# A masked softmax: VectorE's unrolled work put into a loop, and sixteen small writes of the output taken out

## The chip, the cores and the metric

The kernel runs on one core of one Trainium2 chip. The metric is the time of one execution in device microseconds.

## The reference, cut to what matters

```python
batch, heads, seq_q, seq_k = 16, 8, 256, 256
# lengths: 16 integers, each from 128 to 255
for b in range(batch):
    length = lengths[b]
    masked = x[b, :, :, :length]
    e = np.exp(masked - masked.max(-1, keepdims=True))
    result[b, :, :, :length] = e / e.sum(-1, keepdims=True)   # zeros past length
```

A batch is 2048 rows of 256 float32, 2.1 MB, and lies in SBUF as 128 partitions of 16 rows. Input and output are 33.6 MB each; the kernel reads only the columns that a batch needs, rounded up to a width.

## The kernel before

There are eight slots for batches in SBUF. SyncE issues the loads of the first four batches and all stores, GpSimd issues the loads of the later twelve (each of a width picked by the length). VectorE clips what lies past the length to a huge negative number, ScalarE takes the exponential and the row sums, VectorE takes the reciprocals and multiplies. The parts that the argument touches:

```python
# the small writes: one piece of 64 bytes in each of 16 places of the first batch's output
nc.vector.memset(touch, 0.0).then_inc(s_zero, 1)
nc.scalar.wait_ge(s_zero, 1)
nc.scalar.dma_start(out=out_e, in_=touch).then_inc(s_touch, 16)
...
# SyncE: the stores; `parts` cuts batches 0 to 9 in a half and two quarters
nc.sync.wait_ge(s_touch, 16)
for b in range(batch):
    s_b = s_st[b % 2]
    for s in parts(b):
        nc.sync.wait_ge(s_out, ...)                  # VectorE has finished this part
        if b >= 2 and s.start == 0:
            nc.sync.wait_ge(s_b, 64 * (b // 2 + 1))  # the store of batch b-2 has landed
        nc.sync.dma_start(out=out_f[b, :, s, :], in_=xt[:, b % slots, s, :])...
...
# VectorE, unrolled over 16 batches
def mask(b, s):
    v_len = length(DVE, word[0:1, 2 * b : 2 * b + 1])    # reads the length into a register
    nc.vector.wait_ge(s_sw[b % 2], 16 * ((b - ahead) // 2 + 1))   # the load has landed
    with nc.vector.If(v_len < mid):
        clip(b, s, 0, mid)
    clip(b, s, mid, seq_k).then_inc(s_min, ...)
def divide(b, h):                                        # h: a half of the batch
    nc.vector.wait_ge(s_exp, 2 * b + h + 1)
    reciprocal(...)  # counts up s_v
    nc.vector.wait_ge(s_v, v)
    multiply(...)    # counts up s_out
```

The softmax here doesn't subtract the row's maximum and nothing guards it: scores larger than these inputs give would overflow.

## Time and profile before

| | before |
|---|---|
| time, median of the first 3 runs | 156.84 us (156.65 to 157.08) |
| span of the profiled run | 155.0 us |
| moved through DMA | 62.08 MB, 400 GB/s over the span |
| VectorE, ScalarE busy | 74%, 68% |
| VectorE's last multiply ends | 137.9 us |

The profile's lines are read in the prediction below.

### The profile page before, as it was taken

The numbers are of one execution on the slowest core, as the hardware profiler recorded it, in microseconds if no ns is written. First come the engines' busy times: TensorE is split into PE (matmuls) and PEld (weight loads), VectorE is DVE, ScalarE is ACT, GpSimd is POOL, SyncE is SP. The second block draws the span as 40 slices with busy tenths as digits, with TensorE's granted clock in tenths as the row PEclk, the third lists the DMA queues.
The fourth block names the chain that finished last, engine by engine and source line by source line (L and its number), as shares of the span: only waits on it lengthen the run. The fifth ranks groups of instructions, "written<-read, shape, count | busy, mean of one in ns | idle before, by whom it ended". The sixth has DMA issues, their size and how long they took to land.

```text
span 155.0 us, 1322 instructions
## 1 busy us (share of the span) xinstructions
PE 0.2 (0%) x1; PEld 0.1 (0%) x1; DVE 115.1 (74%) x85; ACT 105.2 (68%) x514; POOL 19.0 (12%) x25
## 2 busy tenths in 40 slices
PE   0000000000000000000000000000000000000000
PEld 0000000000000000000000000000000000000000
DVE  1249999957999894949889499999894999950000
ACT  3087799993989694793959488989695798800000
POOL 4910031002020201102020112020100000000000
DMA  4999999999999999999999999999999999999993
GB/s 112 421 452 419 444 309 374 417 429 435 403 409 396 411 413 407 429 407 411 410 413 420 404 419 403 408 412 412 425 405 449 420 419 429 440 435 435 416 419 129
DMA packets 10452, 62.08 MB, mean 400 GB/s; under 512 B 930, under 2 KB 1026, under 8 KB 7122
## 3 DMA queue, kind: packets, MB, share of 16 engines
q1 hardware_dynamic: 6336, 41.95, 66.2%
q0 software_dynamic: 4080, 20.12, 32.0%
q14 instruction: 2, 0.02, 0.0%
q10 hardware_dynamic: 34, 0.00, 0.0%
HBM read 28.51 MB, written 33.56 MB: 400 GB/s over the span
## 4 chain that ended last, share of the span: by engine, by line
DMA 66%; DVE 15%; issue 5%; POOLq 2%; SPq 1%; DVEq 0%
DMA xt<-in_x_dram 58%; DVE xt L231 10%; DMA out_dram<-xt 8%; DVE xt L204 5%; DVE inv_sum L228 1%; SPq L117 1%; POOLq L144 0%; POOLq L139 0%; POOLq L101 0%; SPq L119 0%; SPq L127 0%; DVEq L221 0%; POOLq L166 0%; POOLq L162 0%; POOLq L168 0%
## 5 line engine op out<-in xcount | busy, mean ns | idle before, releaser
L258 ACT ACTIVATE xt<-xt x256 | 102.4, 401 | 27.7 <-DVE xt L204 27.7
L231 DVE TENSOR_TENSOR xt<-xt,inv_sum 128x2048 f32<-128x2048 f32 x32 | 73.3, 2292 | 1.1
L204 DVE SCALAR_TENSOR_TENSOR xt<-down,len_s,xt 128x2048 f32<-128x2048 f32 (+1 forms) x17 | 37.8, 2224 | 18.3 <-DMA xt<-in_x_dram 18.2
L258 ACT ACTIVATION_READ_ACCUMULATOR xt<-xt x256 | 47.9, 187 | 0.0
L139 POOL DMA_DIRECT2D xt<-in_x_dram x12 | 12.8, 1064 | 90.0 <-DMA out_dram<-xt 50.4
L228 DVE RECIPROCAL inv_sum<-row_sum 128x8 f32<-128x8 f32 x32 | 6.3, 196 | 1.1 <-ACT xt L258 1.1
L158 POOL MEMSET xt<- 128x1536 f32 x4 | 5.3, 1386 | 1.1 <-DVE len_s L195 1.1
L250 ACT ACT_TABLE_LOAD x1 | 1.3, 1283 | 2.1 <-DVE touch L112 2.1
L112 DVE MEMSET touch<- 16x16 f32 x1 | 0.1, 72 | 1.2 <-SPq L79 1.2
L187 DVE TENSOR_SCALAR down<-iota_i 128x256 f32<-128x256 int32 x1 | 0.3, 297 | 0.3 <-POOL iota_i L150 0.3
L192 DVE CAST len_b<-word 1x16 bf16<-1x16 int32 x1 | 0.2, 163 | 0.4 <-DMA word<-in_lengths_dram 0.4
L195 DVE TENSOR_SCALAR len_s<-len_f 128x16 f32<-128x16 f32 x1 | 0.2, 173 | 0.3 <-PE len_f L174 0.3
L150 POOL IOTA iota_i<- 128x256 int32 x1 | 0.3, 331 | 0.6 <-SPq L79 0.6
L155 POOL MEMSET seed<- 1x1 f32 x2 | 0.3, 162 | 0.0
L250 ACT ACTIVATE warm<-const-float32-0.0 128x1 f32<-128x1 f32 x1 | 0.2, 203 | 0.0
L153 POOL MEMSET ones<- 1x128 bf16 x1 | 0.2, 194 | 0.0
L174 PE MATMUL len_f<-len_b,ones 1*128 1x16 bf16 x1 | 0.2, 166 | 2.6 <-DVE len_b L192 2.6
L276 POOL MEMSET const-float32-0.0<- 128x1 f32 x1 | 0.1, 98 | 0.3 <-issue 0.3
L174 PEld LDWEIGHTS len_f<-len_b,ones 1*128 1x128 bf16 x1 | 0.1, 100 | 2.6 <-POOL ones L153 2.6
L276 POOL MEMSET const-bfloat16-1.0<- 128x1 bf16 x1 | 0.1, 99 | 0.0
L276 POOL MEMSET const-uint8-127<- 128x1 uint8 x1 | 0.1, 99 | 0.0
L276 POOL MEMSET const-float32-1.0<- 128x1 f32 x1 | 0.1, 98 | 0.0
(1 smaller groups left out, 0.0 us busy)
## 6 DMA issues: line engine op xcount, KB each, us to landing
out_dram<-xt SPq DMA_DIRECT2D x16, 1024.0 KB
out_dram<-xt SPq DMA_DIRECT2D x20, 512.0 KB
xt<-in_x_dram SPq DMA_DIRECT2D x3, 2048.0 KB, 16.1
out_dram<-xt SPq DMA_DIRECT2D x3, 2048.0 KB
xt<-in_x_dram POOLq DMA_DIRECT2D x3, 1728.0 KB, 16.2
xt<-in_x_dram POOLq DMA_DIRECT2D x2, 2048.0 KB, 16.2
xt<-in_x_dram POOLq DMA_DIRECT2D x2, 1600.0 KB, 14.2
xt<-in_x_dram POOLq DMA_DIRECT2D x2, 1280.0 KB, 13.6
```

Source lines behind the costliest of these rows:

```text
L117: nc.sync.dma_start(out=xt[:, 0, s], in_=x_f[0, :, s]).then_inc(s_ld[h], 16)
L139: nc.gpsimd.dma_start(out=xt[:, slot, :, :w], in_=x_n[:, n, :, :w]).then_inc(s_sw[par], 16)
L150: nc.gpsimd.iota(iota_i, pattern=[[1, seq_k]], base=0, channel_multiplier=0).then_inc(s_iota, 1)
L155: nc.gpsimd.memset(seed[:, par : par + 1], 0.0).then_inc(s_st[par], 64)
L158: nc.gpsimd.memset(xt[:, b, :, low:], 0.0).then_inc(s_fill, 1)
L174: nc.tensor.matmul(len_f, lhsT=ones, rhs=len_b, start=True, stop=True).then_inc(s_lenf, 1)
L204: return nc.vector.scalar_tensor_tensor(out=t, in0=down[:, None, lo:hi].to_broadcast([P, s.stop - s.start, hi - lo]), scalar=len_s[:, b : ...
L228: step(nc.vector.reciprocal(out=inv_sum[:, b, s], in_=row_sum[:, b, s]))
L231: nc.vector.tensor_tensor(out=t, in0=t, in1=inv_sum[:, b, s, None].to_broadcast([P, half, seq_k]), op=ALU.mult,).then_inc(s_out, 1)
L250: nc.scalar.activation(out=warm, in_=nc.const_aps.tensor(0.0, (P, 1), F32), func=EXP)
L258: ins = nc.scalar.activation(out=e, in_=e, func=EXP, accum_out=sum_h[:, bass.ds(i, 1), j])
L276: nc = _bacc.Bacc("TRN2", target_bir_lowering=False, num_devices=1)
```

## The change

The intent is a shorter program: VectorE's work for the later twelve batches stands once, in a loop over pairs of batches, and the small writes go. Cut to its core:

```diff
-        nc.vector.memset(touch, 0.0).then_inc(s_zero, 1)
-        nc.scalar.wait_ge(s_zero, 1)
-        nc.scalar.dma_start(out=out_e, in_=touch).then_inc(s_touch, 16)
 ...
-        nc.sync.wait_ge(s_touch, 16)
 ...
-        def mask(b, s):
-            v_len = length(DVE, word[0:1, 2 * b : 2 * b + 1])
-            ... wait for the load ...
+        def mask(b, slot, s):                      # the caller waits for the load first
+            v_len = length(DVE, word[0:1, one(2 * b)])
 ...
-            nc.vector.wait_ge(s_exp, 2 * b + h + 1)
+            nc.vector.wait_ge(s_exp, 2 * b + (h + 1))      # b a register in the loop
 ...
-        for b in range(batch):
-            if b == 0: divide(0, 0)
-            if b + 1 < batch: mask(b + 1, slice(0, nt))
-            if b > 0: divide(b, 0)
-            divide(b, 1)
+        for b in range(ahead - 1):                 # batches 0 to 2, still unrolled
+            nc.vector.wait_ge(s_ld[b + 2], 16)
+            mask(b + 1, b + 1, whole)
+            ... divide both halves of b ...
+        with nc.Fori(0, (batch - ahead) // 2, 1, engines=[DVE]) as r:
+            for par in range(2):
+                n = 2 * r + (ahead + par)
+                b = 2 * r + (ahead + par - 1)
+                nc.vector.wait_ge(s_sw[par], 16 * r + 16)
+                mask(n, n % slots, whole)
+                for h in range(2):
+                    divide(b, b % slots, h)
```

More of the change, by code (lines that the diff above doesn't have):

```diff
@@ L74 @@
     warm = pool.tile([P, 1], F32, name="warm")
-    few = 16
-    touch = pool.tile([few, few], F32, name="touch")
     seed = pool.tile([1, 2], F32, name="seed")
@@ L82 @@
         s_ones = sem("s_ones")
-        s_touch = sem("s_touch")
-        s_zero = sem("s_zero")
         s_lenb = sem("s_lenb")
@@ L108 @@
         nc.scalar.dma_start(out=word64, in_=lengths[None, :]).then_inc(s_word, 16)
-        out_e = out_f[0].rearrange("(e r) t k -> e r t k", e=few)[:, 0, 0, :few]
-        nc.vector.memset(touch, 0.0).then_inc(s_zero, 1)
-        nc.scalar.wait_ge(s_zero, 1)
-        nc.scalar.dma_start(out=out_e, in_=touch).then_inc(s_touch, 16)
         for h in range(2):
@@ L174 @@
         nc.tensor.matmul(len_f, lhsT=ones, rhs=len_b, start=True, stop=True).then_inc(s_lenf, 1)
-        v = 0
-        def step(ins):
-            nonlocal v
-            v += 1
-            ins.then_inc(s_v, 1)
-        nc.vector.wait_ge(s_iota, 1)
-        step(
-            nc.vector.tensor_scalar(
-                out=down, in0=iota_i, scalar1=0.5, scalar2=-big, op0=ALU.add, op1=ALU.mult
-            )
-        )
+        nc.vector.wait_ge(s_iota, 1)
+        nc.vector.tensor_scalar(
+            out=down, in0=iota_i, scalar1=0.5, scalar2=-big, op0=ALU.add, op1=ALU.mult
+        ).then_inc(s_v, 1)
         nc.vector.wait_ge(s_word, 16)
@@ L193, with one, clip @@
         nc.vector.wait_ge(s_lenf, 1)
-        step(
-            nc.vector.tensor_scalar(
-                out=len_s, in0=len_f, scalar1=big, scalar2=None, op0=ALU.mult
-            )
-        )
-        nc.vector.wait_ge(s_v, v)
-        def clip(b, s, lo, hi):
-            t = xt[:, b % slots, s, lo:hi]
+        nc.vector.tensor_scalar(
+            out=len_s, in0=len_f, scalar1=big, scalar2=None, op0=ALU.mult
+        ).then_inc(s_v, 1)
+        nc.vector.wait_ge(s_v, 2)
+        def one(i):
+            return bass.ds(i, 1)
+        def clip(b, slot, s, lo, hi):
+            t = xt[:, one(slot), s, lo:hi].rearrange("p o t c -> p (o t) c")
             return nc.vector.scalar_tensor_tensor(
@@ L206, in clip @@
                 in0=down[:, None, lo:hi].to_broadcast([P, s.stop - s.start, hi - lo]),
-                scalar=len_s[:, b : b + 1],
+                scalar=len_s[:, one(b)],
                 in1=t,
@@ L211, in clip, with divide @@
             )
-        def mask(b, s):
-            v_len = length(DVE, word[0:1, 2 * b : 2 * b + 1])
-            if b == 0:
-                nc.vector.wait_ge(s_ld[s.start // half], 16)
-            elif b < ahead:
-                nc.vector.wait_ge(s_ld[b + 1], 16)
-            else:
-                nc.vector.wait_ge(s_sw[b % 2], 16 * ((b - ahead) // 2 + 1))
-            with nc.vector.If(v_len < mid):
-                clip(b, s, 0, mid)
-            clip(b, s, mid, seq_k).then_inc(s_min, (s.stop - s.start) // half)
-        def divide(b, h):
-            s = slice(h * half, (h + 1) * half)
-            nc.vector.wait_ge(s_exp, 2 * b + h + 1)
-            step(nc.vector.reciprocal(out=inv_sum[:, b, s], in_=row_sum[:, b, s]))
-            nc.vector.wait_ge(s_v, v)
-            t = xt[:, b % slots, s, :]
+        def mask(b, slot, s):
+            v_len = length(DVE, word[0:1, one(2 * b)])
+            with nc.vector.If(v_len < mid):
+                clip(b, slot, s, 0, mid)
+            clip(b, slot, s, mid, seq_k).then_inc(s_min, (s.stop - s.start) // half)
+        hs = [slice(0, half), slice(half, nt)]
+        whole = slice(0, nt)
+        def divide(b, slot, h):
+            nc.vector.wait_ge(s_exp, 2 * b + (h + 1))
+            inv = inv_sum[:, one(b), hs[h]].rearrange("p o t -> p (o t)")
+            nc.vector.reciprocal(
+                out=inv, in_=row_sum[:, one(b), hs[h]].rearrange("p o t -> p (o t)")
+            ).then_inc(s_v, 1)
+            nc.vector.wait_ge(s_v, 2 * b + (h + 3))
+            t = xt[:, one(slot), hs[h], :].rearrange("p o t c -> p (o t) c")
             nc.vector.tensor_tensor(
@@ L233, in divide @@
                 in0=t,
-                in1=inv_sum[:, b, s, None].to_broadcast([P, half, seq_k]),
+                in1=inv[:, :, None].to_broadcast([P, half, seq_k]),
                 op=ALU.mult,
             ).then_inc(s_out, 1)
-        mask(0, slice(0, half))
-        mask(0, slice(half, nt))
-        for b in range(batch):
-            if b == 0:
-                divide(0, 0)
-            if b + 1 < batch:
-                mask(b + 1, slice(0, nt))
-            if b > 0:
-                divide(b, 0)
-            divide(b, 1)
+        for h in range(2):
+            nc.vector.wait_ge(s_ld[h], 16)
+            mask(0, 0, hs[h])
+        divide(0, 0, 0)
+        for b in range(ahead - 1):
+            nc.vector.wait_ge(s_ld[b + 2], 16)
+            mask(b + 1, b + 1, whole)
+            if b > 0:
+                divide(b, b, 0)
+            divide(b, b, 1)
+        with nc.Fori(0, (batch - ahead) // 2, 1, engines=[DVE]) as r:
[4 more added lines that the diff above has]
+                mask(n, n % slots, whole)
+                for h in range(2):
+                    divide(b, b % slots, h)
+        for h in range(2):
+            divide(batch - 1, slots - 1, h)
         nc.scalar.activation(out=warm, in_=nc.const_aps.tensor(0.0, (P, 1), F32), func=EXP)
```

## The prediction

> **What bounds the kernel now.** I read the page's busy table and its 40 slices first, then the windows view (busy time of each engine and what the DMA engines moved in stretches that I chose), then the queue's own waits, then VectorE's timeline near the end.
>
> ```profile
> PE 0.2 (0%) x1; PEld 0.1 (0%) x1; DVE 115.1 (74%) x85; ACT 105.2 (68%) x514; POOL 19.0 (12%) x25
> ...
> DMA  4999999999999999999999999999999999999993
> ...
> HBM read 28.51 MB, written 33.56 MB: 400 GB/s over the span
> ```
>
> No compute engine is full: VectorE is busy 74%, ScalarE 68%. The 16 DMA engines stand at nine tenths in every slice but the first and the last. So the first hypothesis is that the time is 62.08 MB divided by a rate. The windows view says at which rate, stage by stage (after the stretch: its length, the busy time of PE, PEld, DVE, ACT and POOL, the granted clock, the DMA share, GB/s).
>
> ```profile
> 2.00:4.00 2.00, 0.17 (x1) 0.10 (x1) 0.34 (x2) 1.49 (x2) 0.93 (x1) 1.00 0.96 246
> 4.00:20.00 16.00, 0.00 (x0) 0.00 (x0) 10.92 (x8) 9.94 (x49) 4.40 (x4) 1.00 1.02 433
> 20.00:24.00 4.00, 0.00 (x0) 0.00 (x0) 3.93 (x5) 4.00 (x21) 1.29 (x1) 1.00 0.92 281
> 24.00:125.00 101.00, 0.00 (x0) 0.00 (x0) 86.73 (x61) 80.49 (x399) 11.48 (x11) 1.00 1.02 414
> 125.00:150.00 25.00, 0.00 (x0) 0.00 (x0) 12.80 (x10) 9.28 (x46) 0.00 (x0) 1.00 1.01 430
> ```
>
> Loads alone run at 433 GB/s, loads mixed with stores at 414, stores alone at 430. From 125 us on there is nothing left to load: the last 30 us are stores alone, 25 us times 430 GB/s being 10.75 MB, and 5 us at 193 another 1 MB. That is over five batches of 2.1 MB that stand ready in SBUF and wait for the wire. VectorE's last work ends at 137.9, 17 us before the end. Outside the steady rate only two stretches lose anything: 2 to 4 us, (433-246)*2/433 = 0.9 us, and 20 to 24 us, (433-281)*4/433 = 1.4 us.
>
> The queue's own waits say the same from the store side.
>
> ```profile
> SPq L126 <- DMA out_dram<-xt: 100.5, 14, 11.6
> SPq L127 <- DVE xt L231: 11.6, 6, 4.2
> SPq L124 <- DVE xt L231: 10.2, 1, 10.2
> ```
>
> A store's issue waits 100.5 us in total for the store two batches earlier, and 21.8 us for VectorE, all of that in the first batches, where loads fill the ring anyway. How far VectorE runs ahead at the end is read from two timelines: its own (start, duration; the multiplies that finish batch 13 and batch 15), and that of the store queue (the issue of the store of batch 13 and of the first half of batch 15).
>
> ```profile
> 123.62 2.29 DVE L231 TENSOR_TENSOR xt<-xt,inv_sum 128x2048 f32<-128x2048 f32 x1
> ...
> 135.64 2.29 DVE L231 TENSOR_TENSOR xt<-xt,inv_sum 128x2048 f32<-128x2048 f32 x1
> ```
>
> ```profile
> 134.01 0.36 SPq L127 DMA_DIRECT2D out_dram<-xt  x1
> 143.79 0.37 SPq L127 DMA_DIRECT2D out_dram<-xt  x1
> ```
>
> Batch 13 is finished at 123.62+2.29 = 125.9 and its store goes out at 134.0: 8.1 us of lead. Batch 15 is finished at 137.9 and its first store goes out at 143.8: 5.9 us. So the reader should see that the VectorE lines (15% of the chain of waits) are on that chain by inference only; each could slip by nearly 6 us without moving the end, as long as the store queue holds one batch in flight.
>
> **What the Trainium skill says.** (1) "DMA: Bandwidth & Descriptors", section "Issuing engines are not separate DMA queues": transfers started by any engine run on the same 16 DMA engines and interleave. The trace agrees: while the GpSimd queue loads and the SyncE queue stores, the sum is 414 GB/s, below either alone. (2) "Perfetto Trace Analysis", section "Per-engine timelines": a VectorE instruction is pushed into a wait queue and the sequencer goes on; an instruction of the sequencer itself waits in the sequencer. The old loopless form uses the first: a reciprocal starts at 123.39 and takes 0.19, its multiply, which waits for it, starts at 123.62, so 0.04 us later. In the changed order every wait in the loop hangs on a register instruction instead. (3) "Runtime: NRT & Kernel Launch", section "Instruction fetch mechanics": a taken branch whose target isn't in the fetched window costs a fetch. ScalarE already loops here, and its activations follow each other every 0.40 us across the loop's jump, so the trace shows no such cost for a loop of that size. VectorE's program is 105 instructions after and 166 before by the build, so nothing suggests that the jump back leaves what is held.
>
> **The change, part by part.** *The small writes go.* That is one memset of 0.07 us on VectorE, one issue of 0.36 us on ScalarE's queue, 16 packets of 64 bytes, and SyncE's wait for them. They landed 5.3 us after their issue at 1.67, at 7.0 us; the first store is issued at 14.1. The wait ends 7 us before it is needed: worth 0. ScalarE's table load starts up to a microsecond earlier, with its first activation at 8.14: worth 0.
>
> *The loop.* The work on data is the same: 15 and 2 clips, 32 reciprocals, 32 multiplies of 2.29 us, so VectorE stays at 115 us busy. What is added is sequencer work. First, the length is now read after the wait for the batch instead of before it. A read of a length takes 0.31 to 1.26 us on VectorE, median 0.61 over its 17. It is hidden when VectorE is still busy with a multiply, and exposed when VectorE sits waiting for the load, which it did 10 times, two of these for batch 0. So 8 batches, 0.6 us each, about 5 us. Second, in each of 24 halves in the loop the multiply is dispatched only after the sequencer has seen the reciprocal's semaphore. From a branch's end to the start of the next VectorE instruction the trace has 0.15 us; I take 0.2 us, so 24*0.2 = 4.8 us. Register arithmetic between is 0.04 to 0.11 us a piece by ScalarE's rows and lies mostly beside a running multiply. Sum: some 10 us of VectorE idle time added, or 0.8 us a batch.
>
> Does that reach the end? An unhindered batch takes VectorE 7.1 us (clips at 94.46 and 101.59); with 0.4 for two multiplies it is 7.5. Loads land on the average every 8.1 us (4th at 35.6, 15th at 125.1: 89.5/11). So VectorE still catches up with each load, the delays don't add up, and what is left is the delay within one or two batches: 1 to 2 us against a lead of 6 to 17. Buffers are given free by the stores, not by VectorE. Sum of what the loop does to the end: 0. In the first batches the read behind the wait shifts the first store by perhaps 0.5 us; it is queued behind loads until 23.4 us, when its packets begin, so that too is 0.
>
> Predicted: 156.84 + 0 + 0, **156.8 us**.
>
> **The rivals.** *A. The small writes warm something up.* They have no use in the arithmetic, one for each DMA engine, so someone put them there for the first write's sake. For it: the first reads are slow, 246 GB/s in 2 to 4 us, 0.9 us lost; if first writes pay the same and the writes had prepaid it, their removal costs about 0.9 us, giving 157.7. Against it: the dip at 20 to 24 us, where stores begin, is there in spite of them. If they also took part in that dip, removal gains up to 1.4 us, 155.4; nothing in the profile supports it. I give the cost 20% and the gain 5%. *B. VectorE becomes the bound.* If a register wait costs 0.6 us and not 0.2, a batch takes 7.1+1.2+0.6 = 8.9 us, more than the 8.1 between loads; over 12 batches it falls back by 10 us, 4 beyond the lead: 160 to 161. Against it: ScalarE's loop waits on a register 32 times and nothing near 0.6 us shows. 4%. *C. Fewer instructions to fetch give time back.* Then VectorE must now have stalls between instructions; its timeline has starts 0.02 to 0.04 us apart, so there is nothing to win, and it would be off the path: 156.8.
>
> **Range and chances.** The three runs before lie within 0.43 us. With rival A on both sides I take 155.9 to 157.9. Faster by over 2% (below 153.7) would need 3 us out of a DMA-bound span whose two dips hold 2.3 together: 2%. Slower by over 2% (above 160.0) needs B or a much larger A: 4%. Within 2%: 94%.
>
> **What would show it right or wrong.** Right: 62.08 MB again, the DMA row at nines, 414 and 430 GB/s in the mixed and last stretch; VectorE still near 115 us busy with more idle time before the multiply and the clip; the length reads behind the load's landing; the last multiply at 139 to 140 instead of 137.9, and still earlier than the last stores' issue. Wrong, rival A: a slower stretch just where the first stores run, about 20 to 25 us, and everything after it shifted by as much. Wrong, rival B: the queue waiting for VectorE in the last batches and DMA slices below nine after 125 us. The range fails if the dip near 20 us changes by over a microsecond either way.

## The result, and the profile after

The changed kernel took 157.44 us (median of 4 runs, 157.10 to 157.66) against 156.80 us (4 runs, 156.65 to 157.08): ratio 1.0037 with a 95% interval of 1.0013 to 1.0060. Ratios here and below are the mean time of one kernel's runs over the mean of the other's runs of the same rounds, so they are not quite the ratio of the medians; in the experiments they come out of the recorded times only when the profiled run of the kernel under test is left out. 157.44 lies in the stated range. It is 0.64 us above the stated 156.8, and the interval excludes 1.000, so there was a small thing left to explain.

The page of the changed kernel:

```profile
PE 0.2 (0%) x1; PEld 0.1 (0%) x1; DVE 114.8 (74%) x85; ACT 105.2 (68%) x514; POOL 19.0 (12%) x25
...
DMA  4999999999999999999999999999999999999992
...
HBM read 28.51 MB, written 33.55 MB: 400 GB/s over the span
...
L213 DVE TENSOR_TENSOR xt<-xt,inv_sum (+1 forms) x32 | 73.4, 2292 | 4.1 <-DVE inv_sum L208 1.2
L186 DVE SCALAR_TENSOR_TENSOR xt<-down,len_s,xt 128x2048 f32 (+2 forms) x17 | 37.8, 2223 | 16.0 <-DMA xt<-in_x_dram 10.3
```

The last two lines are VectorE's multiplies and clips: busy us, mean ns of one, and the engine's idle us just before them. On the page of the kernel before they read:

```profile
L231 DVE TENSOR_TENSOR xt<-xt,inv_sum 128x2048 f32<-128x2048 f32 x32 | 73.3, 2292 | 1.1
L204 DVE SCALAR_TENSOR_TENSOR xt<-down,len_s,xt 128x2048 f32<-128x2048 f32 (+1 forms) x17 | 37.8, 2224 | 18.3 <-DMA xt<-in_x_dram 18.2
```

The windows view of the changed kernel, in the same stretches (PE, PEld, DVE, ACT, POOL, granted clock, DMA share, GB/s):

```profile
2.00:4.00 2.00, 0.17 (x1) 0.10 (x1) 0.34 (x2) 1.13 (x2) 0.96 (x1) 1.00 0.94 238
4.00:20.00 16.00, 0.00 (x0) 0.00 (x0) 10.45 (x8) 9.39 (x47) 4.37 (x4) 1.00 1.02 434
20.00:24.00 4.00, 0.00 (x0) 0.00 (x0) 3.97 (x4) 4.00 (x22) 1.44 (x2) 1.00 0.92 283
24.00:125.00 101.00, 0.00 (x0) 0.00 (x0) 86.39 (x62) 80.71 (x399) 11.36 (x11) 1.00 1.02 414
125.00:150.00 25.00, 0.00 (x0) 0.00 (x0) 13.38 (x10) 9.58 (x48) 0.00 (x0) 1.00 1.01 429
```

Stage by stage these are the rates of before, within 2 GB/s from 4 us on. The dip at 20 to 24 us is neither deeper nor shallower without the small writes: 283 GB/s against 281.

What did change is VectorE's pace. Its timeline around the first batch of the loop (start, duration; in brackets the idle time before it):

```profile
36.40 2.35 DVE L186 SCALAR_TENSOR_TENSOR xt<-down,len_s,xt 128x2048 f32 x1 [2.84 <-issue]
38.67 0.19 DVE L208 RECIPROCAL inv_sum<-row_sum  x1
39.07 2.29 DVE L213 TENSOR_TENSOR xt<-xt,inv_sum  x1 [0.20 <-DVE inv_sum L208]
```

And the same place in the kernel before:

```profile
35.83 2.35 DVE L204 SCALAR_TENSOR_TENSOR xt<-down,len_s,xt 128x2048 f32<-128x2048 f32 x1 [2.62 <-DMA xt<-in_x_dram]
38.10 0.20 DVE L228 RECIPROCAL inv_sum<-row_sum 128x8 f32<-128x8 f32 x1
38.33 2.29 DVE L231 TENSOR_TENSOR xt<-xt,inv_sum 128x2048 f32<-128x2048 f32 x1
```

Two things are to be seen. The multiply (`TENSOR_TENSOR`) now starts 0.20 us after its reciprocal's end (38.67+0.19 = 38.86, then 39.07) and not 0.03 (38.10+0.20 = 38.30, then 38.33). And the clip starts later although its batch came earlier. By the chain of waits that load landed at 20.77+14.39 = 35.2 us, so the clip came 1.2 us after it; before it landed at 20.85+14.75 = 35.6 us and the clip came 0.2 us after. The two loads, after and before:

```profile
20.77 14.39 DMA xt<-in_x_dram
```

```profile
20.85 14.75 DMA xt<-in_x_dram
```

The last multiply starts at 136.45 and ends at 138.7 us, 0.8 us later than before. The first store of the last batch is still issued at 143.86 (before 143.79):

```profile
136.45 2.29 DVE L213 TENSOR_TENSOR xt<-xt,inv_sum 128x2048 f32<-128x2048 f32 x1
```

```profile
143.86 0.37 SPq L116 DMA_DIRECT2D out_dram<-xt  x1
```

The store queue's waits for VectorE sum to 20.9 us after and 21.8 before. So in the two profiled executions nothing of VectorE's lateness reached the stores. These two spans, 155.1 and 155.0 us, don't show the 0.6 us at all: the profiled run of the changed kernel happens to be its fastest (157.10 us). What follows therefore rests on the timed rounds.

### The profile page after: what moved, and what is told of

Same layout as the page of the kernel before. It is cut to its first block, busy times and chain, and to the rows that moved or that the text cites. A ratio compares the mean times of both kernels' runs of the same rounds, so it can differ in the third digit from the quotient of the medians.

```text
span 155.1 us, 1472 instructions
## 1 busy us (share of the span) xinstructions
PE 0.2 (0%) x1; PEld 0.1 (0%) x1; DVE 114.8 (74%) x85; ACT 105.2 (68%) x514; POOL 19.0 (12%) x25
## 4 chain that ended last, share of the span: by engine, by line
DMA 68%; issue 11%; DVE 5%; POOLq 2%; DVEq 2%; SPq 1%
DMA xt<-in_x_dram 68%; DVE xt L213 3%; DVE xt L186 2%; DVEq L97 1%; DVE inv_sum L208 1%; POOLq L133 1%; POOLq L128 1%; SPq L107 1%; POOLq L97 0%; SPq L109 0%; DVEq L186 0%; DVEq L208 0%; DVEq L213 0%; POOLq L155 0%; DVEq L211 0%
## 5 line engine op out<-in xcount | busy, mean ns | idle before, releaser
L213 DVE TENSOR_TENSOR xt<-xt,inv_sum (+1 forms) x32 | 73.4, 2292 | 4.1 <-DVE inv_sum L208 1.2
L186 DVE SCALAR_TENSOR_TENSOR xt<-down,len_s,xt 128x2048 f32 (+2 forms) x17 | 37.8, 2223 | 16.0 <-DMA xt<-in_x_dram 10.3
L208 DVE RECIPROCAL inv_sum<-row_sum (+1 forms) x32 | 6.2, 195 | 1.5 <-ACT xt L251 1.5
```

The lines of the kernel that those rows point to most:

```text
L186: return nc.vector.scalar_tensor_tensor(out=t, in0=down[:, None, lo:hi].to_broadcast([P, s.stop - s.start, hi - lo]), scalar=len_s[:, one(b)],
L208: nc.vector.reciprocal(out=inv, in_=row_sum[:, one(b), hs[h]].rearrange("p o t -> p (o t)")).then_inc(s_v, 1)
L213: nc.vector.tensor_tensor(out=t, in0=t, in1=inv[:, :, None].to_broadcast([P, half, seq_k]), op=ALU.mult,).then_inc(s_out, 1)
```

## The experiments

Theory L: the loop's later VectorE costs the 0.6 us. Theory W: the small writes had prepaid something (the prediction's rival A). Theory N: it is scatter. Each set of four kernels ran on one chip beside the same 11 runs of the kernel before. Where the text for one run speaks of the others, it speaks of those of its set.

### The changed kernel again (after_again)

No edit.

> The changed kernel once more, unaltered, in five rounds beside the kernel before, to see whether the 0.4% (0.64 us) of the first comparison is real. Theory N (noise): ratio within 0.998 to 1.002 with 1.000 inside the interval. Any real cause: ratio 1.002 to 1.006 again, the interval above 1.000.

Measured: 157.20 us median of 6 runs (156.90 to 158.08) against 156.82 of 11; ratio 1.0035, interval 1.0008 to 1.0062. It repeats in another set of runs, so plain scatter within a set is unlikely for the change as a whole.

### The loop alone (loop_with_writes, loop_with_writes_2)

The changed kernel with the small writes back:

```diff
+        nc.vector.memset(touch, 0.0).then_inc(s_zero, 1)
+        nc.scalar.wait_ge(s_zero, 1)
+        nc.scalar.dma_start(out=out_e, in_=touch).then_inc(s_touch, 16)
 ...
+        nc.sync.wait_ge(s_touch, 16)
```

> The changed kernel with the small writes of the output put back: the loop alone. Theory W (the small writes had prepaid something): the 0.6 us go away, ratio 0.999 to 1.001, 156.8 us. Theory L (the loop's later VectorE costs it): ratio stays at 1.003 to 1.005, 157.3 to 157.5 us. Theory N: 1.000 and so is everything else in this set.

> The loop with the small writes kept, a second time. Theory W: 0.999 to 1.001. Theory N: within the scatter of the unaltered kernel of the same set.

Measured: 156.97 us, ratio 1.0001 (0.9979 to 1.0023), and in another set 156.97 us, ratio 0.9998 (0.9969 to 1.0027). The loop alone costs nothing that these rounds can see; their intervals reach up to 0.27%, so they speak against theory L at its 0.4%, not against every smaller cost.

### The removal of the writes alone (unrolled_no_writes, unrolled_no_writes_2)

The kernel before with those four lines taken out.

> The kernel before without the small writes: their removal alone. Theory W: ratio 1.003 to 1.006, 157.3 to 157.7 us, and the stretch where stores begin (20 to 25 us) is slower than before. Theory L: ratio 0.999 to 1.001, 156.8 us.

> The kernel before without the small writes, a second time, as the first set left it at 1.0015 with an interval across 1.000 and the idle work on VectorE (1.000) has ruled out lateness of VectorE. Theory W: the removal costs 0.2 to 0.4%, ratio 1.002 to 1.004 again. Theory N (it is scatter between sets of runs): as far from 1.000 as the unaltered kernel is in the same set.

Measured: 157.19 us, ratio 1.0015 (0.9991 to 1.0038), and 157.35 us, ratio 1.0024 (0.9992 to 1.0056). Both lie above 1.000 and neither interval clears it. The second half of theory W's expectation failed outright: the stretch where stores begin did not get slower. Its windows line in the first of the two:

```profile
20.00:24.00 4.00, 0.00 (x0) 0.00 (x0) 3.93 (x5) 4.00 (x21) 1.31 (x2) 1.00 0.94 279
```

That is 279 GB/s, against 281 in the kernel before, 307 in the loop with writes and 311 in the changed kernel's second profile. The dip's depth varies from profile to profile and does not follow the writes.

### The length read before the wait (read_before_wait)

```diff
+                v_len = read(n)
                 nc.vector.wait_ge(s_sw[par], 16 * r + 16)
-                mask(n, n % slots, whole)
+                mask(n, n % slots, whole, v_len)
```

> The changed kernel with each batch's length read moved ahead of the wait for its load, as it stood in the kernel before. Clips then start about 0.2 us after a landing instead of 0.7 to 1.2. Theory L in its form 'the read behind the wait': back to ratio 0.999 to 1.001. Theory L in its form 'the dispatch of the multiply' (0.10 to 0.17 us more per half): stays at 1.002 to 1.005. Theory W: stays at 1.003 to 1.006, as the small writes are absent here.

Measured: 156.87 us, ratio 1.0010 (0.9986 to 1.0033). Taken alone it would favour theory L in its first form. With the loop alone at 1.000 it can hardly be that, and it falls short of what theory W asked for (1.003 to 1.006). It is inconclusive. The edit also did less than was expected of it: in its trace a load lands at 60.13 us and the clip starts at 60.61, 0.5 us later and not 0.2, because the branch and the register arithmetic ahead of the clip still stand behind the wait.

### Idle work on VectorE (slack_1us, slack_2us)

To ask how much lateness is free, an addition whose result nobody uses is put ahead of the clip of batches 1 to 15 in the kernel before; k is 4 or 8:

```diff
+            if s.stop - s.start == nt:
+                d = down[:, None, :].to_broadcast([P, k, seq_k])
+                nc.vector.tensor_tensor(out=idle, in0=d, in1=d, op=ALU.add)
             with nc.vector.If(v_len < mid):
```

> The kernel before with one idle addition of 128x1024 on VectorE ahead of the clip of each of batches 1 to 15, an estimated 1.2 us (half of the 2.29 us of 2048 columns, and a fixed part): more lateness for VectorE than the loop brought (its last multiply ended 0.8 us later, in a second trace 1.8). Theory of the prediction (VectorE has nearly 6 us of lead over the store queue): a batch takes 7.1+1.2 = 8.3 us against 8.1 between loads, the last multiply ends at 141 to 143 us instead of 137.9, and the time stays: ratio 0.998 to 1.004. Theory L (the loop's later VectorE costs the 0.6 us): this larger lateness costs at least as much, ratio 1.004 to 1.015.

> The same with 128x2048, 2.29 us a batch. A batch then takes VectorE 9.4 us, more than the 8.1 between loads, and the lead must run out: about 9 us of start and 16 times 9.4 is 160 us for the last multiply, then 3 to 4 us for the last half batch's store: 162 to 166 us, ratio 1.03 to 1.06. If the time hardly rises here either, the lead is larger than the profile says and the bound was misread.

Measured: with 1.22 us a batch 156.93 us, ratio 1.000 (0.9978 to 1.0023); with 2.29 us a batch 166.35 us, ratio 1.0596 (1.0572 to 1.0619). In the first, VectorE's last multiply and the issues of the last two stores (merged into one line, from 144.41 on) stand so:

```profile
139.72 2.29 DVE L235 TENSOR_TENSOR xt<-xt,inv_sum 128x2048 f32<-128x2048 f32 x1
```

```profile
144.41 1.08 SPq L128 DMA_DIRECT2D out_dram<-xt  x2
```

The multiply ends at 142.0, 4.1 us later than before, and it is free within the interval. The loop brought 0.8 us in its first trace and at most 1.8 in the others (139.7 in loop_with_writes). That refutes theory L at the size of 0.6 us: more lateness than the loop brings costs nothing that shows. In the second, the windows view and the queue's waits (us in total, times, the longest) show the lead spent:

```profile
125.00:150.00 25.00, 0.00 (x0) 0.00 (x0) 24.80 (x18) 16.47 (x82) 0.00 (x0) 1.00 0.71 299
```

```profile
SPq L128 <- DVE xt L235: 66.0, 24, 8.9
```

VectorE is busy 24.80 of 25 us, the DMA engines stand at 0.71 and 299 GB/s, and the stores of this line wait 66.0 us for VectorE, where they waited 11.6 before. The bound passes to VectorE, as rival B would have had it, between 1.2 and 2.3 us a batch. The expectation said 162 to 166 us; the time lies 0.35 us above that range.

### GpSimd's first loads earlier (loads_early)

```diff
-        nc.gpsimd.wait_ge(s_ld[ahead - 1], 16)
+        nc.gpsimd.wait_ge(s_ld[1], 16)
```

> The kernel before with GpSimd's first loads (batches 4 and 5) let go when the second half of batch 0 has landed (8.8 us) and not when batch 2 has (18.6 us). About the dip of 20 to 24 us at 281 GB/s. Theory G (the dip comes with GpSimd's first transfers): it moves to 9 to 14 us, the time stays within 0.5 us. Theory S (it comes with the first stores behind the last loads in one queue): it stays near 20 to 24 us, shallower as the other queue fills it; up to 1.4 us gained, 155.4 to 156.8.

Measured: 156.89 us, ratio 0.9993 (0.9974 to 1.0012). The windows view:

```profile
20.00:24.00 4.00, 0.00 (x0) 0.00 (x0) 3.35 (x3) 3.81 (x20) 0.00 (x0) 1.00 1.03 409
24.00:26.00 2.00, 0.00 (x0) 0.00 (x0) 1.97 (x3) 2.00 (x12) 0.00 (x0) 1.00 0.93 314
```

The dip did not move to GpSimd's first transfers (issued at 11 us; 426 GB/s from 9 to 14 us, 436 before), so theory G of that run fails. Theory S fits in part: the dip did not stay and get shallower, and its gain of up to 1.4 us did not come. It moved from 20 to 24 us to 24 to 26 us (before: 406 there), with the end of the first loads, which now share the engines with GpSimd's. Filling the old place gained (409-281)*4 us = 0.5 MB, but the time did not follow: 314 against 406 in 24 to 26 us gives back 0.2 MB of it, and 412 against 434 in 14 to 20 us and 421 against 428 in 26 to 40 us another 0.1 MB each. A dip in a rate view is not yet a gain.

### Wider stores (wide_stores)

```diff
-            cuts = [0, half, half + quarter, nt]
+            cuts = [0, half, nt]
```

> The kernel before with the stores of the first ten batches cut in halves, none in quarters, to see what a real lever on this bound is. Descriptors of 4096 bytes take 159 ns, of 8192 bytes 309 ns in the trace of before, so 10.5 MB of the stores go 3% faster: 10.5 MB / 16 engines / 8192 bytes is 80 pairs of descriptors, 9 ns each, 0.7 us. If the bound is the bytes' rate: 156.1 us, ratio 0.994 to 0.998. If the later start of a half's store matters: 1.000 or above.

Measured: 159.75 us, ratio 1.0169 (1.0147 to 1.0191). I was wrong in sign. The queue's waits, the end of the windows view, and the last batch's clip:

```profile
SPq L127 <- DVE xt L231: 89.5, 26, 8.7
```

```profile
125.00:150.00 25.00, 0.00 (x0) 0.00 (x0) 21.77 (x17) 17.52 (x88) 0.00 (x0) 1.00 0.90 379
```

```profile
137.53 2.35 DVE L204 SCALAR_TENSOR_TENSOR xt<-down,len_s,xt 128x2048 f32<-128x2048 f32 x1 [0.69 <-DMA xt<-in_x_dram]
```

The last batch is clipped at 137.5 and not at 125.8 us, because its load came 12 us later. The store queue then waits 89.5 us for VectorE, the stretch from 125 us runs at 379 GB/s and not 430, and the end is starved. The rate from 26 to 125 us is 413 GB/s against 414, so the bytes were not slower. They went in another order: stores first, loads late. The DMA view from 26 to 125 us shows it (q1 is SyncE's queue, by then stores alone, q0 is GpSimd's loads; packets, MB, share of the 16 engines), before and then here:

```profile
q1 hardware_dynamic: 4309, 20.89, 51.8%
q0 software_dynamic: 4080, 20.12, 50.1%
```

```profile
q1 hardware_dynamic: 3240, 23.56, 57.5%
q0 software_dynamic: 3754, 17.33, 44.0%
```

The Trainium skill, "DMA: Bandwidth & Descriptors", section "Queues, rings and completion order", says that each engine goes round the queues that have work, packet by packet. This run agrees with it: with twice the bytes in the packets of a batch's second half, the stores got 23.6 MB in place of 20.9 and the loads 17.3 in place of 20.1, in the same 99 us. The quarters in the kernel before are what keeps the loads, and with them VectorE's lead, ahead.

### A control, and more small writes (before_again, writes_everywhere)

> The kernel before, unaltered, counted as a kernel of its own beside the runs of before: the control for what a ratio of two equal kernels shows here. Expected 0.999 to 1.001; if it is 0.997 or 1.003, differences of 0.3% cannot be given to any part of the change.

> The kernel before with the small writes put not into the first batch's output alone but into all sixteen, 256 packets in place of 16. Theory W, if the first write to each region costs something: ratio 0.996 to 0.999, and no dip near 20 to 24 us or a shallower one. Theory W, if it is only each engine's first write: 0.999 to 1.001. Theory N: 0.999 to 1.001.

The second has this edit:

```diff
-        out_e = out_f[0].rearrange("(e r) t k -> e r t k", e=few)[:, 0, 0, :few]
+        out_e = out_f.rearrange("b (e r) t k -> e b r t k", e=few)[:, :, 0, 0, :few]
 ...     # the source is broadcast over the 16 batches
```

Measured: the unaltered kernel against itself 157.09 us, ratio 1.0010 (0.9979 to 1.0041), so a thousandth, with an interval of 0.3% to either side, is what one pair of equal kernels showed. Writes into every batch's output: 156.90 us, ratio 0.9998 (0.9971 to 1.0025). More of them gain nothing, so if they prepay anything it is not by region of the output.

### What the timed runs say together

| kernel | small writes | ratio to before |
|---|---|---|
| the change, first and second set | no | 1.0037, 1.0035 |
| unrolled, no writes, two sets | no | 1.0015, 1.0024 |
| read before wait | no | 1.0010 |
| the loop with writes, two sets | yes | 1.0001, 0.9998 |
| the kernel before against itself | yes | 1.0010 |
| idle work 1.2 us, early loads, writes everywhere | yes | 1.0000, 0.9993, 0.9998 |

I took every single run's time less the mean of the runs of before of its own set. The 28 runs without the small writes (five groups in three sets) average +0.35 us, with a standard error of 0.08; the 36 runs with them average +0.02 us, with 0.05. The grouping was made after the results were seen, and a set's runs share one mean of before, so it is weaker than it looks. It favours theory W: the removal of the writes, not the loop, carries 0.2 to 0.4% where it carries anything. It does not show how. One slow run without the writes was profiled, unrolled_no_writes (157.92 us, span 155.9). It keeps the rates of before up to 150 us (414 in the mixed stage, 429 to 150 us) and differs at the very end. From 153 to 154 us the kernel before, then slack_1us, then unrolled_no_writes show:

```profile
153.00:154.00 1.00, 0.00 (x0) 0.00 (x0) 0.00 (x0) 0.00 (x0) 0.00 (x0) 1.00 0.00 0
153.00:154.00 1.00, 0.00 (x0) 0.00 (x0) 0.00 (x0) 0.00 (x0) 0.00 (x0) 1.00 0.04 16
153.00:154.00 1.00, 0.00 (x0) 0.00 (x0) 0.00 (x0) 0.00 (x0) 0.00 (x0) 1.00 0.06 25
```

25 GB/s over 1 us is 25 KB, three packets of 8 KB. Leaving out wide_stores and slack_2us, four of the twelve profiles have such stragglers, with spans of 155.3 to 155.9 us, and the other eight, of at most 155.1 us, have none. Three of the four kernels have the small writes (slack_1us, loop_with_writes, before_again). So a late tail of single packets goes with the slower profiled runs, and these traces do not tie it to the writes; whether their absence makes it more frequent was not tested. Theory N remains possible for the removal alone, as the control lies at 1.0010 itself.

## Why the prediction was right

**The bound.** Right. The bytes and the rates by stage are unchanged (414 in the mixed stage, 429 against 430 at the end), and so is the time within 0.4%.

**The loop: VectorE slower, the end unmoved.** Right, and shown: the loop alone gives 1.0001 and 0.9998, and 4.1 us of extra lateness gives 1.000. The terms of the sum were of the right kind, with sizes off. The wait of the multiply for its reciprocal was put at 0.2 us more in 24 halves, 4.8 us. The timeline shows 0.14 to 0.20 us from end to start in place of 0.03, and VectorE's idle time before the multiplies rose from 1.1 to 4.1 us, so 3.0. The register operation that carries this wait takes 53 to 115 ns, median 65. The exposed read of the length was put at 0.6 us a batch; at the one batch followed above the clip came 1.2 us after the landing in place of 0.2. Of this the read took 0.52; the rest is the branch and register arithmetic, which the prediction took to lie beside a running multiply. A batch without hindrance takes 7.36 us (clips at 94.88 and 102.24) where 7.5 was said. The last multiply was to end at 139 to 140 us and ended at 138.7.

The sum of some 10 us of added idle time did not come. Idle time before the clips was to grow and fell, from 18.3 to 16.0 us, as a VectorE that comes later to a load waits less for it. Before multiplies, clips and reciprocals together it rose from 20.5 to 21.6. The prediction's other argument, that VectorE catches up with each load and the delays don't add up, is what held. Its count of VectorE's program, 105 instructions after and 166 before, stands in no view; a build of the two files here gave 166 before and 177 after, 81 of these register arithmetic that the compiler partly joins. Nothing in the sum rests on it.

**The lead of nearly 6 us.** Right as far as tested: 4.1 us of slip was free. The second idle addition let the last multiply end at 156.5 us, 18.6 us later, and cost 9.4 us. So the edge lies between 4.1 and 18.6 us of slip, and the 6 itself was not measured.

**The small writes: worth 0.** This is the step that may have been mis-sized. The prediction gave a cost of 0.9 us a chance of 20%. The removal alone measured +0.15% and +0.24%, some 0.2 to 0.4 us, each not clear of zero. The place where rival A would have shown itself, a slower stretch at 20 to 25 us, stayed as it was. The step's reasoning (the writes' wait ends 7 us before it is needed) stands for the wait; whether the writes do something else is open.

**What stays open.** The whole change costs 0.35 to 0.37% in two sets, the removal alone 0.15 to 0.24%, the loop alone nothing. Whether the remaining tenth is scatter or the two parts need each other is below what these rounds resolve. None of the kernels tried beats the kernel before by a clear margin.

## What to carry to other kernels

When the DMA row stands at nine tenths everywhere, find how far ahead of the store queue each engine finishes; a change that slows an engine within that lead is free, and one idle instruction per batch, in two sizes, brackets the lead by experiment. Before widening a store's pieces, ask what share of the DMA engines the loads will lose to it. Differences of 0.3% need a control of the kernel against itself.

## What the Trainium skill lacked or had wrong

- No page that I found gives what a wait against a register costs between two VectorE instructions. "Perfetto Trace Analysis", section "Per-engine timelines", has the mechanism (an instruction of the sequencer waits in the sequencer), and the trace agrees, with a register operation of 53 to 115 ns in each gap; the number here is 0.14 to 0.20 us from a reciprocal's end to its multiply's start, against 0.03 us for a wait in the queue.
- "DMA: Bandwidth & Descriptors", section "Latency and other measured facts", gives about 600 ns as the floor of a register's load (`tensor_load`). Here such reads, of a word in SBUF, took VectorE 305 ns at the least, with a median of 611, and 1258 at the most (17 reads in the kernel before; in the changed kernel 308, 353 and 1389).
- The same page has the turn-taking between queues but not its consequence: with stores cut in halves and not in quarters, the loads got 17.3 MB in place of 20.1 between 26 and 125 us, the last load landed 12 us later and the kernel took 1.7% longer.
- "Advanced Engine Details and Errata", section "Control Flow Timing", has about 108 ns for a compare-and-branch; VectorE's took 56 ns in the profile here (17 of them, 56 to 63); the page does not say whether its figure holds more than what the profile records.
